# The prompt's output projection and final norm, moved from the attention of the samples to the end of the input projections

## The chip, the cores and the metric

The kernel runs on one core of one Trainium2 chip. The metric is device time in microseconds of a whole call. In the text PE is the matrix engine (TensorE), PEld its weight load, DVE the vector engine, ACT the scalar engine, POOL GpSimd, and SP the engine whose queue issues nearly all DMAs here.

## The reference

Two layers work on 256 prompt rows and 2048 sample rows of width 1024. Layer 0 is a convolution, layer 1 attention. What matters here is the end of layer 1 for the prompt:

```
q, k, v, z = split(h @ na_w_in)                     # prompt: 256 rows, sample: 2048 rows
att  = context_attention(q, k, v)                   # prompt, 16 heads of 64
out  = (att * silu(z)) @ na_w_out                   # 1024 x 1024 weights
x    = x + gate * out                               # gate of the prompt: from c_ctx
y_prompt = rms_norm(x, final_g)
# the sample rows: the same with neighbourhood attention and another gate
y_sample = rms_norm(x_s + gate_s * ((att_s * silu(z_s)) @ na_w_out), final_g)
```

Everything is f32. A product of two f32 matrices is made of three f32r matmuls: each operand is split into a rounded half (h) and the rest (l), and h\*h, h\*l and l\*h are added up in PSUM.

## The kernel before

**Stages.** `phase1` does layer 0, the input projections of layer 1 (`na_values`, `na_rest`) and the attention of the prompt (`prompt_attention`). `phase2` does the attention of the samples (`attention`) with the output projections woven in. Intermediate results go through scratch in HBM: queries `qh_d`/`ql_d`, keys `ks_d`, the SiLU branch `zn_d`, the prompt's gated attention `yp_d`, and the gated, split output weights `w2_d`.

**The end of the input projections.** `na_rest` yields 24 parts (eight column blocks `ct`, in each a key, a query and a SiLU part, numbered 1, 0, 3). A part is 24 matmuls of 128x512 on each of two blocks of 512 rows and 24 of 128x256 on a block of 256 rows. In profile rows these matmuls are `ni_s`, lines L356 to L358. Their PSUM bank is emptied by ACT (`ni_s_f`, `ni_s_h`), and the results are stored by SP from a ring of six `st` tiles.

**What is woven in there.** `weave` and `mixed` set the order in which the program is written: beside eight parts run the generators `prompt_attention` (eight pairs of heads, tiles `pa_*`, the last store is `yp_d<-pa_yl`), `gated_weights` and `context_values` (tiles `cv`). `gated_weights` reads `na_w_out`, multiplies it by both gates (DVE), rounds it (ACT), takes the rest (DVE) and stores four quarters for each of eight row blocks and two gates into `w2_d`. A scheduler then moves instructions within this stretch, by the estimates that it makes of each engine; the order of each engine is fixed in the program, and SP's DMAs are issued in that order.

**The hand-over.** When the prompt's attention is done, its memory is given back, and `start_attention` loads the first two heads of the samples (`a_k`, `a_bm`, `a_qh`, `a_ql`, `ck`, `cv`, `a_v`, `a_z`) while the last three parts of `na_rest` are computed.

**phase2.** 64 heads (two halves `hg` of eight heads, four groups `G` of 512 rows) of four units each make 256 units. A unit has four score matmuls (`sa_S`), softmax, eight transposes (`sa_T`), and in every second unit the product with the values (`sa_O`). PE and DVE keep the order that `attention` writes. `out_group` is the output projection of a group: for each tile of 128 rows and each half of the columns 12 matmuls, in two chunks of six; `side_chunk` puts one chunk into a unit where there is one in `chunks`. The weights are read from `w2_d` into `w2h`/`w2l` by `load_w2` (1 MB each, four buffers), the first ones at the steps W2_STEPS. At step BEGIN = 20 two groups for the prompt (`G` is None) come ahead of all others: they read `yp_d` (`yp_0h`, ...), use their own weights, and the weights of the samples are loaded after them. `while self.tiles_left + nt > 7` in `head_out` empties the list of chunks at once when too many tiles wait. Where PE's names in the order below have `sa_3_1_S`, this is head 3, unit 1 of a group.

Of the kernel before, what the change touches and what calls it, by code (L numbers as in the profile page):

```python
# [18 lines left out]
P = 128  # L19
D = 1024  # L20
# [28 lines left out]
BEGIN = 20  # L49
WAIT = 3  # L50
NEAR = 3
W2_STEPS = 8, 14
# [24 lines left out]
class Kern:  # L77
    def __init__(self, ctx, tc, io):
        self.tc, self.nc, self.io = tc, tc.nc, io
        self.ctx = ctx  # L80
        self.more, self.turn = None, 0
# [16 lines left out]
        self.w2_d = d("w2_d", [2, 2, D, D])  # L98
# [25 lines left out]
    def mm_bank(self, name, tag="mm"):  # L124
        if self.more and tag == "mm":
            self.turn = (self.turn + 1) % 3
            if self.turn:
                return self.more.tile([P, 512], F32, tag=tag, name=name, bufs=4)
        return self.ps.tile([P, 512], F32, tag=tag, name=name)
# [1021 lines left out]
    def gated_weights(self):  # L1151
# [3 lines left out]
        gate = [self.spread_row(work(f"gate1_{g}"), self.gate_d[1, g]) for g in range(2)]  # L1155
        for k in range(NK):
# [3 lines left out]
            for g in range(2):  # L1160
                for i in range(2):
                    cs = slice(512 * i, 512 * i + 512)
                    t, hi = (self.bp.tile([P, 512], dt, tag="out", name=f"w2_{k}{g}{i}{s}", bufs=4) for dt, s in ((F32, "t"), (F32R, "h")))
                    lo = t.bitcast(F32R)
                    nc.vector.tensor_tensor(out=t, in0=raw[:, cs], in1=gate[g][:, cs], op=ALU.mult)
                    nc.scalar.copy(hi, t)
                    self.rest_dve(lo, t, hi)
                    nc.sync.dma_start(self.w2_d[g, 0, rows, cs], hi.bitcast(F32))
                    nc.sync.dma_start(self.w2_d[g, 1, rows, cs], lo.bitcast(F32))
                    yield  # L1170
# [99 lines left out]
    def phase1(self):  # L1270
        tc = self.tc
        with ExitStack() as c:
# [34 lines left out]
            with tc.tile_pool(name="bp", bufs=1, side="right") as self.bp:  # L1307
                with tc.tile_pool(name="mb", bufs=1, side="right") as self.mb, tc.tile_pool(name="more", bufs=1, space=bass.MemoryType.PSUM) as self.more:
                    side = itertools.chain(self.context_keys(), self.masked_bias())
# [57 lines left out]
    def attention(self):  # L1367
# [10 lines left out]
        for i in range(-1, len(units) + 4):  # L1378
            self.step = i
            if i in W2_STEPS:  # L1380
                self.load_w2(0, 0, W2_STEPS.index(i), True)
            if i == BEGIN:
                for hg in range(2):
# [384 lines left out]
```

## Time and profile before

| | |
|---|---|
| median of 3 runs | 2831.47 us (2831.18 to 2834.06) |
| the profiled execution's own time | 2833.08 us |
| its span, first to last instruction | 2831.3 us |
| mean granted clock of PE | 0.985 |
| PE busy / DVE / ACT / POOL | 95% / 65% / 51% / 53% of the span |
| DMA | 548.02 MB, mean 194 GB/s |
| first score matmul of the samples (start of phase2 on PE) | 1822.96 us |

The page gives the busy time of each engine, the span in 40 slices with the granted clock and the DMA share, the chain of work that ended last, and the costliest groups of instructions. The views used below are the table of stretches (busy microseconds of each engine in a stretch, then the granted clock, the share of the 16 DMA engines, and GB/s), the list of waits (engine and line, who released it, microseconds in total, times, longest), the instructions in order of time (start, duration, engine, line), the groups by line (count, busy microseconds, mean ns, idle time before) and the chain.

### The profile page before, as it was taken

The numbers are of one execution on the slowest core, as the hardware profiler recorded it, in microseconds if no ns is written. First come the engines' busy times: TensorE is split into PE (matmuls) and PEld (weight loads), VectorE is DVE, ScalarE is ACT, GpSimd is POOL, SyncE is SP. The second block draws the span as 40 slices with busy tenths as digits, with TensorE's granted clock in tenths as the row PEclk, the third lists the DMA queues.
The fourth block names the chain that finished last, engine by engine and source line by source line (L and its number), as shares of the span: only waits on it lengthen the run. The fifth ranks groups of instructions, "written<-read, shape, count | busy, mean of one in ns | idle before, by whom it ended". The sixth has DMA issues, their size and how long they took to land.

```text
span 2831.3 us, 45475 instructions
## 1 busy us (share of the span) xinstructions
PE 2694.4 (95%) x16079; PEld 2329.6 (82%) x16079; DVE 1851.7 (65%) x3154; ACT 1450.6 (51%) x2546; POOL 1505.6 (53%) x1631
## 2 busy tenths in 40 slices
PE   6999999999899999999999989989899999899998
PEld 4888877776677888999998878778788898788887
DVE  4789989999886510023456542277487787778885
ACT  4457565677544312233212254266476676667774
POOL 5679878888663343354213334145455555455564
PEclk9999999999899999999999999999999999999999
DMA  7233554555435554446789996799777767966753
GB/s 255 84 119 113 188 179 159 188 177 181 155 120 165 165 157 129 132 144 224 238 295 348 342 298 213 199 239 240 225 207 198 198 181 197 247 189 180 199 168 109
DMA packets 435627, 548.02 MB, mean 194 GB/s; under 512 B 42945, under 2 KB 306201, under 8 KB 435272
## 3 DMA queue, kind: packets, MB, share of 16 engines
q1 hardware_dynamic: 430080, 522.17, 61.9%
q10 hardware_dynamic: 5320, 22.95, 2.1%
q8 instruction: 128, 2.10, 0.3%
q14 instruction: 99, 0.81, 0.1%
HBM read 359.86 MB, written 189.22 MB: 194 GB/s over the span
## 4 chain that ended last, share of the span: by engine, by line
PE 67%; DMA 12%; DVE 7%; SPq 4%; ACT 4%; POOL 2%; issue 2%; POOLq 0%; ACTq 0%; DVEq 0%
PE sa_T L1527 7%; PE ci_ps L356 6%; PE ci_ps L357 6%; PE ci_ps L358 6%; PE sa_O L1556 5%; PE sa_O L1551 4%; PE sa_S L1495 3%; PE sa_S L1494 3%; PE ni_s L356 3%; PE ni_s L357 3%; PE ni_s L358 3%; PE o L1658 2%; PE o L1660 2%; PE o L1659 2%; DVE cv L507 2%
## 5 line engine op out<-in xcount | busy, mean ns | idle before, releaser
L1521 POOL TENSOR_SCALAR sa_p<-sa_p,sa_m 128x992 f32<-128x992 f32 (+2 forms) x256 | 279.2, 1091 | 442.2 <-DVE sa_m L1520 319.0
L507 DVE SCALAR_TENSOR_TENSOR cv<-u,dw,cv 128x640 f32<-128x640 f32 (+2 forms) x570 | 427.8, 821 | 3.8 <-ACT cv L503 2.9
L1536 ACT CAST sa_pt<-sa_T 128x512 fp32r<-128x512 f32 (+3 forms) x512 | 275.3, 588 | 224.9 <-PE sa_T L1527 223.3
L112 DVE TENSOR_TENSOR sa_pt<-sa_T,sa_pt 128x512 fp32r<-128x512 f32 (+3 forms) x512 | 328.4, 682 | 3.3 <-ACT sa_pt L1536 3.0
L356 PE MATMUL ci_ps<-h_s_hi,ci_wh 128*128 128x512 f32 x768 | 306.6, 399 | 1.8 <-DVE shift L244 1.0
L358 PE MATMUL ci_ps<-h_s_hi,ci_wl 128*128 128x512 f32 x768 | 303.1, 395 | 0.0
L357 PE MATMUL ci_ps<-h_s_lo,ci_wh 128*128 128x512 f32 x768 | 302.7, 394 | 0.0
L1513 DVE TENSOR_REDUCE sa_m<-sa_S 128x1 f32<-128x512 f32 x256 | 176.1, 688 | 190.0 <-PE sa_S L1495 175.3
L1519 ACT ACTIVATE sa_p<-sa_S,sa_m 128x992 f32<-128x992 f32 (+2 forms) x256 | 267.3, 1044 | 56.1 <-DVE sa_m L1515 47.6
L1527 PE MATMUL sa_T<-ident,sa_p 128*128 128x128 f32 (+3 forms) x2048 | 272.6, 276 | 9.1 <-DVE sa_pt L112 8.7
L1527 PEld LDWEIGHTS sa_T<-ident,sa_p 128*128 128x128 f32 (+3 forms) x2048 | 239.3, 138 | 44.8 <-issue 14.0
L488 POOL TENSOR_TENSOR cv_s<-cv_s,cv_p 128x519 f32<-128x519 f32 (+1 forms) x155 | 233.3, 1505 | 69.6 <-DVE cv_s L511 46.9
L485 ACT ACTIVATE cv_p<-u,dw 128x640 f32<-128x640 f32 (+2 forms) x326 | 241.0, 770 | 55.0 <-POOL cv_s L488 35.8
L488 POOL TENSOR_TENSOR cv_p<-cv_p,cv_p 128x520 f32<-128x520 f32 (+1 forms) x155 | 227.8, 1470 | 26.6 <-ACT cv_p L485 18.9
L1556 PE MATMUL sa_O<-sa_pt,a_v 120*128 120x256 f32 (+5 forms) x1280 | 190.2, 278 | 0.0
L1551 PE MATMUL sa_O<-sa_pt,cv 128*128 128x256 f32 x1024 | 175.2, 293 | 3.6 <-ACT sa_pt L1536 0.8
L356 PEld LDWEIGHTS ci_ps<-h_s_hi,ci_wh 128*128 128x128 f32 x768 | 145.4, 189 | 39.1 <-ACT cv_p L485 2.5
L1515 DVE CUSTOM_DVE_ANT_0 sa_S<-sa_S,a_bm,sa_m 128x480 f32<-128x480 f32 (+2 forms) x256 | 170.9, 668 | 9.1
L358 PEld LDWEIGHTS ci_ps<-h_s_hi,ci_wl 128*128 128x128 f32 x768 | 144.9, 189 | 33.6
L357 PEld LDWEIGHTS ci_ps<-h_s_lo,ci_wh 128*128 128x128 f32 x768 | 145.2, 189 | 31.0
L1556 PEld LDWEIGHTS sa_O<-sa_pt,a_v 120*128 120x128 f32 (+2 forms) x1280 | 167.0, 191 | 0.0
L356 PE MATMUL ni_s<-h_s_hi,nis_wh 128*128 128x512 f32 x384 | 151.2, 394 | 8.4 <-DVE ni_s_l L112 5.4
(849 smaller groups left out, 7186.4 us busy)
## 6 DMA issues: line engine op xcount, KB each, us to landing
adaw<-in_ada_w SPq DMA_DIRECT2D x24, 1024.0 KB
ci_w<-in_conv_w_in SPq DMA_DIRECT2D x48, 512.0 KB
a_bm<-bm_d SPq DMA_DIRECT2D x32, 720.0 KB
x_s<-in_x_sample SPq DMA_DIRECT2D x32, 512.0 KB
vs_d<-v_s SPq DMA_DIRECT2D x128, 128.0 KB
a_qh<-qh_d SPq DMA_DIRECT2D x128, 128.0 KB
a_ql<-ql_d SPq DMA_DIRECT2D x128, 128.0 KB
o_x<-x_d SPq DMA_DIRECT2D x32, 512.0 KB
```

Of the source, the lines that this page charges most:

```text
L112: self.nc.vector.tensor_tensor(out=lo, in0=src, in1=hi.bitcast(F32), op=ALU.subtract)
L356: self.nc.tensor.matmul(out, wh[:, k, :], hh[:, k, :], start=k == 0, stop=False)
L357: self.nc.tensor.matmul(out, wh[:, k, :], hl[:, k, :], start=False, stop=False)
L358: self.nc.tensor.matmul(out, wl[:, k, :], hh[:, k, :], start=False, stop=k == NK - 1)
L488: nc.gpsimd.tensor_tensor(out=st["sum", half], in0=st["sum", half], in1=st[half, tap], op=ALU.add)
L507: nc.vector.scalar_tensor_tensor(out=out, in0=u, scalar=w, in1=first, op0=ALU.mult, op1=ALU.add)
L1519: nc.scalar.activation(p[:, n], S[:, n], AF.Exp, scale=-1.0, bias=m[:, 2:3], accum_out=m[:, 3:4])
L1521: nc.gpsimd.tensor_scalar(out=p[:, n], in0=p[:, n], scalar1=m[:, 3:4], scalar2=1.0, op0=ALU.mult, op1=ALU.mult)
L1527: nc.tensor.transpose(t[:w, c * P : c * P + P], p[:, x + c * w : x + c * w + w], self.ident)
L1536: nc.scalar.copy(pt[:w, 0, part, :, at], t)
L1551: nc.tensor.matmul(o, cv[:, c].rearrange("p s d -> p (s d)"), x, start=s + c == 0, stop=False)
L1556: nc.tensor.matmul(dst, v[:w, c0 + c].rearrange("p s d -> p (s d)"), loc[:, lo:hi], start=False, stop=s == 1 and c == 3)
```

## The change

The two prompt groups leave `phase2`. A new generator, `prompt_out`, does the prompt's whole output projection, residual and final norm in `phase1`, right behind `prompt_attention`, beside two parts of `na_rest`. It reads `na_w_out` itself in 16 pieces of 128x512, gates and splits each on the way (`gated`: DVE, ACT, DVE) and multiplies at once, so `gated_weights` makes and stores only the samples' weights. The prompt's attention is woven into six parts in place of eight. The first weights of the samples are loaded at steps 14 and 22 in place of the prompt's at 8 and 14.

```diff
-BEGIN = 20
-W2_STEPS = 8, 14
+W2_STEPS = 14, 22
...
-            self.turn = (self.turn + 1) % 3
+            self.turn = (self.turn + 1) % (1 + self.more_bufs // 2)
...
     def gated_weights(self):
...
-            for g in range(2):
-                for i in range(2):
...
+            for i in range(2):
+                cs = slice(512 * i, 512 * i + 512)
+                t, hi = (self.bp.tile([P, 512], dt, tag="out", name=f"w2_{k}{i}{s}", bufs=4) for dt, s in ((F32, "t"), (F32R, "h")))
+                self.gated(t, hi, t.bitcast(F32R), raw[:, cs], gate[:, cs])
+                nc.sync.dma_start(self.w2_d[0, rows, cs], hi.bitcast(F32))
+                nc.sync.dma_start(self.w2_d[1, rows, cs], t)
+                yield
+    def gated(self, t, hi, lo, raw, gate):
+        self.nc.vector.tensor_tensor(out=t, in0=raw, in1=gate, op=ALU.mult)
+        self.nc.scalar.copy(hi, t)
+        self.rest_dve(lo, t, hi)
+    def prompt_out(self, pool, ps):
+        nc, io = self.nc, self.io
+        T = lambda tag, dt, n, bufs, name="": pool.tile([P, n], dt, tag=tag, name=f"po_{tag}{name}", bufs=bufs)
+        gate = self.spread_row(T("gate", F32, D, 1), self.gate_d[1, 0])
+        fg = self.spread_row(T("fg", F32, D, 1), io["final_g"])
+        y, x = [], []
+        for k in range(NK):
+            t = pool.tile([P, 2, NPR], F32R, tag="y", name=f"po_y{k}", bufs=NK)
+            nc.sync.dma_start(t.bitcast(F32), self.yp_d[k].rearrange("s p t -> p s t"))
+            y.append(t)
+        todo = [(h, k) for h in range(2) for k in range(NK)]
+        def weights(h, k):
+            cs = slice(h * 512, h * 512 + 512)
+            raw, t, hi, lo = (T(tag, dt, 512, bufs, f"{h}{k}") for tag, dt, bufs in (("raw", F32, 3), ("t", F32, 2), ("hi", F32R, 3), ("lo", F32R, 3)))
+            nc.sync.dma_start(raw, io["na_w_out"][0, k * P : k * P + P, cs])
+            self.gated(t, hi, lo, raw, gate[:, cs])
+            return hi, lo
+        ahead = [weights(*todo.pop(0)) for _ in range(2)]
+        for u in range(2):
+            x.append(T("x", F32, D, 2, str(u)))
+            nc.sync.dma_start(x[u], self.x1_d[u * P : u * P + P, :])
+        yield
+        for h in range(2):
+            cs = slice(h * 512, h * 512 + 512)
+            pm = [ps.tile([P, 512], F32, tag="po", name=f"po_{h}{u}", bufs=2) for u in range(2)]
+            for k in range(NK):
+                wh, wl = ahead.pop(0)
+                for u in range(2):
+                    yh, yl = (y[k][:, s, u * P : u * P + P] for s in range(2))
+                    nc.tensor.matmul(pm[u], yh, wh, start=k == 0, stop=False)
+                    nc.tensor.matmul(pm[u], yh, wl, start=False, stop=False)
+                    nc.tensor.matmul(pm[u], yl, wh, start=False, stop=k == NK - 1)
+                yield
+                if todo:
+                    ahead.append(weights(*todo.pop(0)))
+                yield
+            for u in range(2):
+                nc.vector.tensor_tensor(out=x[u][:, cs], in0=pm[u], in1=x[u][:, cs], op=ALU.add)
+            yield
+        for u in range(2):
+            r = self.rms_scale(x[u], f"po_n{u}")
+            nc.vector.scalar_tensor_tensor(out=x[u], in0=x[u], scalar=r, in1=fg, op0=ALU.mult, op1=ALU.mult)
+            nc.sync.dma_start(io["y_prompt"][0, u * P : u * P + P, :], x[u])
+        yield
...
-                    side = self.mixed(self.prompt_attention(pq, pps), side, 40 / 52)
-                    self.weave(itertools.islice(rest, 8), side, 14.5)
+                    side = self.mixed(self.prompt_attention(pq, pps), side, 24 / 52)
+                    self.weave(itertools.islice(rest, 6), side, 13)
                     for _ in side:
                         pass
             extra.close()
+            with tc.tile_pool(name="po", bufs=1, side="right") as po, tc.tile_pool(name="pops", bufs=1, space=bass.MemoryType.PSUM) as pps, tc.tile_pool(name="more2", bufs=1, space=bass.MemoryType.PSUM) as self.more:
+                self.more_bufs = 2
+                side = self.prompt_out(po, pps)
+                self.weave(itertools.islice(rest, 2), side, 18)
+                for _ in side:
+                    pass
+            self.more = None
             self.start_attention()
...
-            if i == BEGIN:
-                for hg in range(2):
-                    self.chunks.append(self.out_group({"hg": hg, "G": None}))
-                    self.due += 4 * NPR // P + WAIT
-                    self.tiles_left += NPR // P
```

**SP, end of the prompt's attention.** Before (line 1244 stores `yp_d`, lines 1450 and on load the first head of the samples):

```order
L1244 DMA yp_d<-pa_yh 128x256
L1087 DMA ql_d<-ni_0_s_l 128x4x64
L1244 DMA yp_d<-pa_yl 128x256
L1011 DMA zn_d<-ni_3_s_f 128x512
L1450 DMA a_0_k<-ks_d 128x704
L1455 DMA a_0_bm<-bm_d 128x3x352
L1459 DMA a_0_qh<-qh_d 64x512 x2
```

The same place in the changed program, and what stands there ahead of the samples' first load (lines 1294, 249, 1183, 1190 and 1503 are `yp_d`, gate, `yp_d` read back, `na_w_out` and the first head):

```order
L1294 DMA yp_d<-pa_yl 128x256
L249 DMA po_gate<-gate_d 128x1024
L249 DMA po_fg<-in_final_g 128x1024
L1183 DMA po_y_16729<-yp_d 128x2x256
...
L1190 DMA po_raw_17049<-in_na_w_out 128x512
L1010 DMA zn_d<-ni_3_s_f 128x512 x2
L1219 DMA out_y_prompt<-po_x_16761 128x1024
L1219 DMA out_y_prompt<-po_x_16763 128x1024
L1010 DMA zn_d<-ni_3_s_f 128x256
L1503 DMA a_0_k<-ks_d 128x704
```

Between the last store of the prompt's attention and the samples' first load stand now the 30 DMAs of `prompt_out` and ten stores of the projections.

**ACT, last column block of the projections.** Before, the SiLU parts that empty PSUM (line 1010) follow one another:

```order
L1010 ACTIVATE ni_3_s_f<-ni_3_s_16888 128x256
L1010 ACTIVATE ni_3_s_f<-ni_3_s_16967 128x512
L1010 ACTIVATE ni_3_s_f<-ni_3_s_16995 128x512
L1010 ACTIVATE ni_3_s_f<-ni_3_s_17023 128x256
L1106 CAST ni_1_s_h<-ni_1_s_17057 128x512
```

In the changed program (line 1170 rounds the prompt's weights, line 257 squares its rows for the norm, line 1009 is the SiLU):

```order
L1009 ACTIVATE ni_3_s_f<-ni_3_s_16943 128x256
L1170 CAST po_hi_16789<-po_t_16788 128x512
...
L1170 CAST po_hi_17051<-po_t_17050 128x512
L257 ACTIVATE po_n_sq,po_n_r<-po_x_16761 128x1024
L257 ACTIVATE po_n_sq,po_n_r<-po_x_16763 128x1024
L1009 ACTIVATE ni_3_s_f<-ni_3_s_17135 128x512
L1009 ACTIVATE ni_3_s_f<-ni_3_s_17163 128x512
```

The banks 17135 and 17163 of the last SiLU part are emptied only behind the prompt's last 13 weights and the squares of its norm. On PE the third block of that part, bank 17191, comes right behind the last matmul of `prompt_out`, and the SiLU part has two banks:

```order
L1207 MATMUL po_16972<-po_lo_17052,po_y_16743 128x512
L1208 MATMUL po_16972<-po_hi_17051,po_y_16743 128x512
L355 MATMUL ni_3_s_17191<-h_s_hl,nis_7_3_wh 128x256
L356 MATMUL ni_3_s_17191<-h_s_hl,nis_7_3_wh 128x256
```

Of the 96 prompt matmuls 48 stand in this order in a row behind the second block of that part; the other 48 are mixed with projection matmuls.

**PE in phase2.** In units 24 to 37 the eight prompt chunks of the first half are gone. Of the second half, 12 are gone from units 43 and 44, and of the 66 matmuls of unit 45 there remain 30, those of the samples' group 0. Nothing else in the order of PE in phase2 differs.

More of the change, by code (lines that the diff above doesn't have):

```diff
@@ L80, in __init__ @@
         self.ctx = ctx
-        self.more, self.turn = None, 0
+        self.more, self.more_bufs, self.turn = None, 0, 0
         self.cp = ctx.enter_context(tc.tile_pool(name="consts", bufs=1))
@@ L125, in mm_bank @@
         if self.more and tag == "mm":
-            self.turn = (self.turn + 1) % 3
+            self.turn = (self.turn + 1) % (1 + self.more_bufs // 2)
             if self.turn:
-                return self.more.tile([P, 512], F32, tag=tag, name=name, bufs=4)
+                return self.more.tile([P, 512], F32, tag=tag, name=name, bufs=self.more_bufs)
         return self.ps.tile([P, 512], F32, tag=tag, name=name)
@@ L1154, in gated_weights @@
         work = lambda name: self.xp.tile([P, D], F32, tag="ln", name=name, bufs=5)
-        gate = [self.spread_row(work(f"gate1_{g}"), self.gate_d[1, g]) for g in range(2)]
+        gate = self.spread_row(work("gate1"), self.gate_d[1, 1])
         for k in range(NK):
@@ L1159, in gated_weights @@
             nc.sync.dma_start(raw, self.io["na_w_out"][0, rows, :])
-            for g in range(2):
-                for i in range(2):
[L1162 to L1170, printed above, removed]
+            for i in range(2):
[5 more added lines that the diff above has]
+                yield
@@ L1601, in head_out, with load_w2 @@
             self.put_off(3 + u, lambda u=u: split(u))
-    def load_w2(self, hg, g, h, hold=False):
-        if hg > 1:
-            return
-        w = [self.T("w2", [P, 4, 512], F32R, f"w2{s}{hg}{g}{h}") for s in "hl"]
+    def load_w2(self, hg, h, hold=False):
+        w = [self.T("w2", [P, 4, 512], F32R, f"w2{s}{hg}{h}") for s in "hl"]
         for s in range(2):
-            src = self.w2_d[g, s, hg * 512 : hg * 512 + 512, h * 512 : h * 512 + 512]
+            src = self.w2_d[s, hg * 512 : hg * 512 + 512, h * 512 : h * 512 + 512]
             if hold:
@@ L1613, in load_w2 @@
             self.nc.sync.dma_start(w[s].bitcast(F32), src.rearrange("(k p) n -> p k n", p=P))
-        self.w2.setdefault((hg, g), []).append(w)
+        self.w2.setdefault(hg, []).append(w)
     def out_group(self, grp):
         nc, T, hg, G = self.nc, self.T, grp["hg"], grp["G"]
-        g = 0 if G is None else 1
-        w = self.w2[hg, g]
+        w = self.w2[hg]
         if hg and self.fg is None:
             self.fg = self.spread_row(T("row", [P, D], F32, "final_g"), self.io["final_g"])
-        out = self.io["y_prompt" if G is None else "y_sample"][0]
-        base = 0 if G is None else NPR + G * 512
-        o0 = 0 if G is None else G * 512
-        if G is None:
-            grp["y"] = [tuple(T("y", [P, 4, P], F32R, f"yp{hg}_{u}{s}") for s in "hl") for u in range(NPR // P)]
-            for u, y in enumerate(grp["y"]):
-                for s, t in enumerate(y):
-                    self.hold(t[:, 0, 0:1])
-                    nc.sync.dma_start(t.bitcast(F32), self.yp_d[4 * hg : 4 * hg + 4, s, :, u * P : u * P + P].rearrange("c p t -> p c t"))
-        if G is None or G == 0:
+        out = self.io["y_sample"][0]
+        base = NPR + G * 512
+        o0 = G * 512
+        if G == 0:
             for _ in range(WAIT):
```

9 lines of the change are left out of this document (5 added, 4 removed).

## The prediction

> **What bounds the kernel now.** I read the page first, then stretches around the two places that the change touches, then the waits in them.
>
> ```profile
> PE 2694.4 (95%) x16079; PEld 2329.6 (82%) x16079; DVE 1851.7 (65%) x3154; ACT 1450.6 (51%) x2546; POOL 1505.6 (53%) x1631
> ```
>
> PE is the bound, so a matmul that is only moved is worth nothing by itself. A gain must come from PE's idle time, and the table of stretches shows where there is some.
>
> ```profile
> 1620.00:1740.00 120.00, 105.22 (x577) 89.77 (x576) 44.47 (x74) 57.76 (x130) 40.93 (x50) 0.97 0.90 286
> 1740.00:1820.00 80.00, 80.00 (x437) 69.61 (x436) 13.69 (x22) 20.12 (x40) 24.45 (x28) 1.00 0.69 189
> 1955.50:2035.00 79.50, 64.33 (x352) 52.04 (x350) 39.19 (x83) 35.85 (x65) 30.88 (x38) 0.94 0.85 245
> ```
>
> The reader sees the duration, the busy time of PE first, and at the end clock, DMA share and GB/s. Where the prompt's attention runs (1620 to 1740) PE idles 14.8 us under nearly full DMA engines; behind it, where the output projection now goes, PE has no hole. In phase2 between 1955.5 and 2035 it idles 15.2 us. The waits name the causes:
>
> ```profile
> PE ni_s L356 <- DVE ni_s_l L112: 5.4, 2, 3.2
> PE ni_s L356 <- ACT ni_s_f L1010: 3.7, 1, 3.7
> ...
> PE o_None L1658 <- DMA yp_0h<-yp_d: 5.6, 1, 5.6
> PE o L1659 <- DMA w2l<-w_d: 2.1, 1, 2.1
> ```
>
> The first two are of 1615 to 1740 (emptying of PSUM, held up behind stores), the last two of 1955 to 2035: the prompt's second half waits for its data, and the samples' group for weights that load only when the prompt's are done with. These two causes leave the program.
>
> **What phase2 gives back.** Units are counted by `sa_S` (four each), output matmuls by `w2h` (two of three). Three tables over the same stretches: all engines, `sa_S`, `w2h`.
>
> ```profile
> 1833.70:1858.10 24.40, 23.05 (x171) 20.72 (x169) 21.57 (x54) 18.27 (x35) 8.73 (x9) 1.00 0.75 199
> 1903.60:1955.40 51.80, 51.08 (x345) 45.96 (x344) 41.63 (x94) 34.95 (x65) 26.37 (x40) 1.00 0.86 220
> 1966.50:2098.30 131.80, 117.48 (x704) 99.78 (x703) 81.52 (x170) 72.46 (x131) 59.28 (x78) 0.96 0.79 221
> 2115.40:2215.60 100.20, 99.53 (x656) 88.49 (x655) 77.83 (x169) 67.75 (x123) 51.39 (x70) 1.00 0.68 184
> 2468.00:2571.50 103.50, 100.72 (x656) 88.18 (x655) 80.98 (x169) 70.74 (x127) 55.70 (x75) 1.00 0.65 179
> ...
> 1833.70:1858.10 24.40, 8.10 (x32) 1.00 0.75 199
> 1903.60:1955.40 51.80, 14.68 (x56) 1.00 0.86 220
> 1966.50:2098.30 131.80, 31.18 (x108) 0.96 0.79 221
> 2468.00:2571.50 103.50, 30.56 (x108) 1.00 0.65 179
> ...
> 1903.60:1955.40 51.80, 11.63 (x32) 1.00 0.86 220
> 1966.50:2098.30 131.80, 36.57 (x96) 0.96 0.79 221
> 2468.00:2571.50 103.50, 23.29 (x64) 1.00 0.65 179
> ```
>
> First term. Units 24 to 37 (1903.6 to 1955.4, 14 units) hold 48 prompt matmuls. Without them they are like units 4 to 11 (1833.7 to 1858.1), which hold no output chunk: 24.4 / 8 = 3.05 us each, 14 x 3.05 = 42.7, a gain of 9.1. The matmuls themselves would be 11; the rest stays, since DVE is then busy 21.57 of 24.40 us. Bounds: 0, if loads set the pace there (below), to 9.1.
>
> Second term. Units 41 to 67 (27 units) take 131.8 us with 144 output matmuls. The changed program has 96 there, in the same pattern as units 169 to 195 of the second half (103.5 us, one burst of 30, first chunks of a group): a gain of 28.3. Against the 27 units at 2115.4 (100.2 us) it is 31.6, but those have no burst, so I take 28.3. It holds 11 us of matmuls, the idle time and the slower clock behind it (0.96 against 1.00).
>
> Sum for phase2: -37.4 us (bounds -28.3 and -40.7). The prompt's emptying, adds, squares and scales on ACT, POOL and DVE, its `yp` and weight loads, its stores and its x loads leave with it; their cover was PE, so they add nothing. What is late next is the pace of DVE and PE themselves.
>
> **What phase1 pays.**
>
> ```profile
> 1717.36 0.39 PE L356 MATMUL ni_s<-h_s_hi,nis_wh 128*128 128x512 f32 x1
> 1720.08 0.39 PE L356 MATMUL ni_s<-h_s_hi,nis_wh 128*128 128x512 f32 x1
> 1727.33 0.58 PE L356 MATMUL ni_s<-h_s_hl,nis_wh 128*128 128x256 f32 x1 [3.69 <-ACT ni_s_f L1010]
> 1729.84 0.41 PE L358 MATMUL ni_s<-h_s_hl,nis_wl 128*128 128x256 f32 x1
> 1730.23 0.28 PE L357 MATMUL ni_s<-h_s_hl,nis_wh 128*128 128x256 f32 x1
> 1730.91 0.28 PE L357 MATMUL ni_s<-h_s_hl,nis_wh 128*128 128x256 f32 x1
> ```
>
> (1) Matmuls: twelve of 128x512 start within 2.72 us, 0.227 each; 96 x 0.227 = +21.8, with no idle PE to cover them. Six of 128x256 take 0.68 us when warm (0.113), and 11 take 2.51 right behind a gap of 3.69 us: such a gap costs another 1.3 us.
>
> (2) The first prompt matmul. It needs the last pair's `yp_d` landed, then gate, norm weights, eight `y` and a piece of weights, through SP in this order.
>
> ```profile
> 1766.89 0.64 PE L1231 MATMUL pa_O<-pa_pt,pa_v 128*128 128x256 f32 x4
> ...
> 1773.79 0.32 SPq L1244 DMA_DIRECT2D yp_d<-pa_yl  x1
> 1775.64 0.32 SPq L1450 DMA_DIRECT2D a_k<-ks_d  x1
> ...
> 1801.26 0.47 SPq L1115 DMA_DIRECT2D ks_d<-ni_s_h  x1
> ...
> 1822.96 0.50 PE sa_S L1494
> ```
>
> From the last `pa_O` (end 1767.53) to the load behind the landing are 8.1 us. The loads are 2 x 0.52 + 8 x 0.26 = 3.1 MB, 11.0 us at the 286 GB/s above; the weights 0.9 more; multiplication 0.71 and rounding 0.62 (rows below) 1.3: 21.3 us. The new order of PE has 72 matmuls of 128x512 and 39 of 128x256 between the two: 16.3 + 4.4 = 20.7. A wait of 0.6; I take 1 (0 to 10, the upper end when each step doubles its row: not sooner). SP's issues lie under the transfers: in the rows above it issues 24 loads of the samples and five stores in 25.6 us.
>
> (3) The stream of weights. Three `raw` buffers: a piece can be had each (landing + 1.3) / 3. PE uses one in six matmuls, 1.36 us; in the second 48 nothing covers it.
>
> ```profile
> L1165 DVE TENSOR_TENSOR w_510t<-w,gate 128x512 f32<-128x512 f32 x1 | 0.7, 707 | 3.6 <-DMA w_d<-w_500h 3.6
> L1146 ACT CAST cv<-cv 128x512 fp32r<-128x512 f32 x8 | 4.7, 617 | 11.5 <-DMA cv<-in_cache_v 11.2 <-DVE w_701t L1165 0.4
> ...
> 702.22 3.66 DMA co_raw<-in_conv_w_out
> ...
> 1682.84 8.50 DMA cv<-in_cache_v
> 1713.74 6.19 DMA cv<-in_cache_v
> ```
>
> The rows of the chain are landings of 512 KB, quiet and crowded; a piece is 256 KB. At 3.66 us: 1.65 per piece, 8 x 0.29 = 2.3; at 8.50: 3.27, 8 x 1.9 = 15. Beside it the DMA share is like 1740 to 1820 (0.69), so the quiet row is nearest: +2 (0 to 15). DVE's two passes per piece, 1.4 us, keep pace with PE. On SP the stores of the SiLU part are queued behind pieces that wait for a `raw` buffer; their `st` tiles are wanted again only at the hand-over (5), so nobody waits for them here. The DVE and ACT work of gating is as much as before, half of it moved here, beside matmuls.
>
> [...]
>
> (4) ACT's order. The third block of the last SiLU part waits for a bank that ACT empties behind the prompt's two squares.
>
> ```profile
> L1679 DVE TENSOR_TENSOR o_x<-o,o_x 128x512 f32<-128x512 f32 x9 | 6.2, 688 | 3.8 <-PE o L1660 3.7
> ...
> L258 ACT ACTIVATE o_sq<-o_x 128x1024 bf16<-128x1024 f32 x6 | 6.3, 1056 | 20.9 <-DVE o_x L1679 20.9
> L258 ACT ACTIVATION_READ_ACCUMULATOR o_sq<-o_x 128x1 f32 x6 | 1.1, 187 | 0.0
> ```
>
> From the last prompt matmul: one add 0.7, two squares 2 x 1.24, one SiLU of the size of the rounding 0.6: 3.8 us of wait, and 1.3 of slow clock: +5 (3 if the first add starts early).
>
> [...]
>
> (5) The hand-over. Before, the samples' first loads took SP from 1775.64 to 1801.26, 25.6 us, with 47 us of projections left (to 1822.96). Now they are issued about 8 us behind the last prompt matmul (squares, scales, two stores), the `ks_d` stores behind them at about 34 us, and PE has 3.8 + 2.7 + 13.6 + 10.9 = 31 us until it needs a bank whose ACT copy waits for those stores (ring of six `st`): a wait of about 3. +3 (0 to 9).
>
> (6) Less DMA in the tail. 32 stores of 256 KB fewer, 8.4 MB, 29 us of DMA at 286 GB/s; the loads and stores of `cv`, which stand in the chain at 1683 and 1714 ahead of PE's waits, come earlier. The idle 14.8 us and 3.6 of slow clock (120 x 0.03) can go: at most -18; the prompt's attention, in six parts now, keeps its own dependences. I take -10 (-4 to -18).
>
> Sum for phase1: 21.8 + 1 + 2 + 5 + 3 - 10 = +22.8. With phase2: -14.6. Against the profiled execution's own 2833.1 that is 2818.5; the median of runs is 1.6 lower, so 2817.
>
> **Rivals.** A, slower: the DMA engines stay full through the prompt's projection. Place: the second 48 matmuls. Price: weights landing in 8.50 us cost 15 instead of 2, the first wait 10 instead of 1, and the tail is relieved of 4 instead of 10: -14.6 + 13 + 9 + 6 = +13, 2845. At a landing of 6.19 it is (2.5 - 1.36) x 8 = 9, with half of the others about +0: between the two it decides. For it speaks the share of 0.90 up to 1740; against it 0.69 behind, and the stores that go.
>
> B, no change: phase2 gives back less. The first weights of the samples come at steps 14 and 22, into units without output matmuls, where heads are used faster.
>
> ```profile
> PE sa_S L1494 <- DMA ck<-kc_d: 6.3, 1, 6.3
> ```
>
> This wait, between 1860 and 1900, comes behind the two pairs of weight loads of steps 8 and 14. If loads set the pace in units 14 to 37, 7 of the first term's 9.1 stay and such a wait comes once more: -14.6 + 7 + 6.3 = -1, 2830.
>
> C, much faster: terms 2, 3 and 5 are hidden, term 6 is 18, and phase2 gives 40.7: 21.8 + 5 - 18 - 40.7 = -32, 2800.
>
> That the work stays in phase2 or is pulled elsewhere is excluded by the order shown.
>
> **How the numbers follow.** The likeliest case 0.60, A 0.10, B 0.15, C 0.15. The range 2802 to 2834 leaves out A and the far half of C, and takes in B. A measurement of this kernel tells about 0.2% (5.7 us) from no change: the likeliest case and C are faster (0.75), B is the same (0.15), A slower (0.10).
>
> **What would show it.** In the profile after: the first `sa_S` about 23 us later than 1822.96; from it to the end 37 us less than before; no wait of PE for `yp`, and 27 units from the 41st in about 103 us (term two); 14 units from the 24th in 43 us (term one); a wait of PE's `ni_s` of about 4 us behind the last `po` matmul, released by ACT (term 4); PE's waits in the tail below 5 us (term 6); landing of the weights in the second 48 matmuls (term 3). It is wrong if PE waits for `po_hi` or `po_lo` again and again, or if the units from 24 on wait for loads.

## The result, and the profile after

The changed kernel takes 2819.59 us (median of six runs, 2811.96 to 2821.11) against 2833.55 us for the kernel before on the same chip: a ratio of 0.9945, 95% interval 0.9931 to 0.9959. The forecast was 2817 within 2802 to 2834, so the time came out as forecast. Two of its steps did not come out where they were said to, and the profile shows which. The profiled execution took 2820.92 us (span 2819.1 us).

The engines' line of the page of the changed kernel:

```profile
PE 2692.4 (96%) x16079; PEld 2328.8 (83%) x16079; DVE 1849.1 (66%) x3150; ACT 1446.6 (51%) x2538; POOL 1488.6 (53%) x1623
```

PE has the same 16079 matmuls as before and, within 2 us, the same busy time; what went is for the most part idle time. Some instructions of the changed kernel on PE in order of time: the first of the 96 prompt matmuls, the first and the last of the second 48, then the projection behind them, the last wait of the projections, and the first score matmul of the samples.

```profile
1772.37 0.63 PE L1206 MATMUL po<-po_hi,po_y 128*128 128x512 f32 x2
...
1795.35 0.39 PE L1206 MATMUL po<-po_hi,po_y 128*128 128x512 f32 x1
...
1806.02 0.39 PE L1208 MATMUL po<-po_hi,po_y 128*128 128x512 f32 x1
...
1809.44 0.38 PE L355 MATMUL ni_s<-h_s_hl,nis_wh 128*128 128x256 f32 x1 [3.03 <-ACT ni_s_f L1009]
...
1842.19 0.58 PE L355 MATMUL ni_s<-h_s_hl,nis_wh 128*128 128x256 f32 x1 [3.55 <-ACT ni_s_f L1017]
...
1848.24 0.51 PE L1547 MATMUL sa_S<-ck,a_qh 128*128 128x512 f32 x1 [0.55 <-ACT ni_s_f L1017]
...
1938.89 0.77 PE L1547 MATMUL sa_S<-ck,a_qh 128*128 128x512 f32 x1 [5.38 <-DMA ck<-kc_d]
```

The first `sa_S` comes at 1848.24 us in place of 1822.96: 25.3 us later. From there to the end of the span it is 970.9 us in place of 1008.3: 37.4 us less. The second 48 prompt matmuls start within 10.67 us, 47 steps of 0.227, without a wait. The next two rows show two waits of PE that the kernel before did not have, and the last one a wait for context keys.

Stretches of the changed kernel (duration, busy time of PE first, at the end clock, DMA share and GB/s). The third begins at the last matmul of `na_values`, which stands ahead of all that the change touches on PE, and ends at the first `sa_S`; the last three are units 0 to 23, 24 to 37 and 41 to 67:

```profile
1500.00:1620.00 120.00, 113.90 (x593) 97.55 (x592) 74.18 (x102) 31.71 (x52) 36.91 (x24) 1.00 1.00 355
1620.00:1740.00 120.00, 118.14 (x683) 104.10 (x682) 37.74 (x64) 55.84 (x129) 51.77 (x68) 1.00 0.79 233
1453.65:1848.24 394.59, 379.50 (x2020) 328.16 (x2018) 172.00 (x254) 124.15 (x244) 122.66 (x120) 0.99 0.84 268
1848.24:1920.96 72.72, 65.09 (x453) 57.37 (x453) 61.11 (x151) 51.65 (x95) 32.80 (x49) 0.98 0.89 240
1920.96:1972.11 51.15, 43.52 (x298) 38.27 (x296) 40.78 (x92) 33.21 (x61) 21.33 (x35) 0.93 0.86 213
1983.17:2086.74 103.57, 100.78 (x657) 88.21 (x655) 78.16 (x169) 68.05 (x123) 51.77 (x70) 1.00 0.66 180
```

Two stretches of the kernel before that the prediction did not show, for the first and the third row:

```profile
1500.00:1620.00 120.00, 119.84 (x633) 103.43 (x632) 79.39 (x112) 31.32 (x52) 39.60 (x28) 1.00 1.00 347
1449.06:1822.96 373.90, 358.40 (x1924) 308.67 (x1922) 167.50 (x248) 121.33 (x240) 121.93 (x116) 0.99 0.88 283
```

The reader sees three things. In the tail (1620 to 1740) PE idles 1.9 us in place of 14.8 and the clock is 1.00 in place of 0.97. Ahead of it (1500 to 1620) it idles 6.1 us in place of 0.2. And measured from a point that both programs reach in the same way, the end of the projections costs 394.6 - 373.9 = 20.7 us; the other 4.6 of the 25.3 had passed ahead of that point (1453.65 against 1449.06). It came at anything from 1449 to 1457 us in the 13 profiles of this case, with the same order of PE up to it, so a single span can't be read closer than that.

### The profile page after: what moved, and what is told of

The parts are those of the page before. It is cut to its first block, busy times and chain, and to the rows that moved or that the text cites. A ratio compares the mean times of both kernels' runs of the same rounds, so it can differ in the third digit from the quotient of the medians.

```text
span 2819.1 us, 45421 instructions
## 1 busy us (share of the span) xinstructions
PE 2692.4 (96%) x16079; PEld 2328.8 (83%) x16079; DVE 1849.1 (66%) x3150; ACT 1446.6 (51%) x2538; POOL 1488.6 (53%) x1623
## 4 chain that ended last, share of the span: by engine, by line
PE 69%; DMA 10%; DVE 7%; SPq 4%; ACT 3%; POOL 3%; issue 2%; POOLq 0%; ACTq 0%; DVEq 0%
PE sa_T L1580 7%; PE ci_ps L355 6%; PE ci_ps L356 5%; PE ci_ps L357 5%; PE sa_O L1609 5%; PE sa_O L1604 4%; PE sa_S L1548 4%; PE sa_S L1547 4%; PE ni_s L356 4%; PE ni_s L357 4%; PE ni_s L355 4%; DMA bm_d<-bm 2%; PE o L1702 2%; PE o L1704 2%; PE o L1703 2%
```

## The experiments

Lines of rows can differ by up to nine between these kernels, since the edits add lines.

**One: the samples' weights later.** Units 24 to 37 lost 5.4 us to a wait for `ck` behind the weight loads. Do they collide, or do all loads together set the pace?

```diff
-W2_STEPS = 14, 22
+W2_STEPS = 30, 36
```

> The changed kernel with the samples' first weights at steps 30 and 36 in place of 14 and 22, nothing else. Theory (a collision): only the first group of heads loads context keys, and the wait of 5.4 us for ck in unit 27 comes because four loads of 1 MB stand ahead of those keys on the queue; behind the last key they meet nothing. Then the waits for ck in units 19 and 27 (1.1 and 5.4 us) are gone, units 0 to 37 take 117 to 118 us in place of 123.9, and the run is 6 to 7 us shorter, about 2813. Rival (the pace of all loads, rival B of the prediction): the bytes of units 14 to 45 are the same, so a wait of 4 us or more comes back in units 28 to 46 for keys, queries or w2h, and the time stays within 2 us of 2819.6.

2818.58 us, ratio 0.9943 (0.9928 to 0.9957). The total can't tell it from the changed kernel, and the 6 to 7 us of the expectation did not come; the profile tells them apart. Units 24 to 37 of this kernel, and the only wait of PE for a load from the first `sa_S` up to 1990 us:

```profile
1919.20:1966.38 47.18, 43.02 (x297) 37.82 (x295) 41.08 (x98) 33.26 (x62) 23.27 (x39) 0.96 0.97 244
```

```profile
PE sa_S L1548 <- DMA a_ql<-ql_d: 2.0, 1, 2.0
```

The wait for `ck` is gone. So is the 1.1 us of unit 19, which the expectation put down to `ck` and the profile to ACT (`sa_pt`); it had cost nothing, since units 0 to 23 take 72.7 us in both. Units 0 to 37 take 119.9 us in place of 123.9: 4.0 won, not 6 to 7, because 2.0 come back as a wait for queries in unit 36, behind the first pair of weights. So it was a collision for the most part, and the pace of the loads for the rest.

**Two: the old steps.** This separates the two constants from the removal of the prompt's chunks.

```diff
-W2_STEPS = 14, 22
+W2_STEPS = 8, 14
```

> The changed kernel with the steps 8 and 14 of the kernel before in place of 14 and 22. It separates the two constants from the removal of the prompt's chunks. Theory (the wait for ck follows the weights): a wait of about 6 us is back in unit 19 and one of 1 to 1.5 in unit 15, units 0 to 23 take 80 us again (72.7 with steps 14 and 22), units 24 to 37 take 43 to 45 us as the prediction's first term said, and the sum of units 0 to 37 is 123 to 126, the total 2819 to 2822. Rival (the removal made the wait, the steps have no part in it): units 0 to 23 stay at 73, units 24 to 37 at 51.

2810.52 us, ratio 0.9916 (0.9899 to 0.9933). Units 0 to 23 and 24 to 37, and the wait for keys:

```profile
1839.38:1918.25 78.87, 66.68 (x452) 59.49 (x453) 61.52 (x151) 51.64 (x95) 32.78 (x49) 0.94 0.90 244
1918.25:1963.19 44.94, 41.82 (x298) 36.16 (x295) 40.38 (x92) 33.26 (x61) 21.34 (x35) 1.00 0.79 205
```

```profile
PE sa_S L1547 <- DMA ck<-kc_d: 6.5, 2, 5.5
```

The wait is back in unit 19 (5.5 us), units 24 to 37 take 44.9, and the sum is 123.8, as with steps 14 and 22. The steps only choose in which of the two stretches the same wait falls. The total, 9 us below the changed kernel, was not expected (2819 to 2822 was): phase2 as a whole took only 2.2 us less (968.7). Experiments nine and ten come back to it.

**Three: the norm's squares on DVE.** Is the wait of 3.03 us behind the last prompt matmul ACT's order?

```diff
-            r = self.rms_scale(x[u], f"po_n{u}")
+            r = self.rms_dve(x[u], f"po_n{u}")
...
+        nc.vector.tensor_tensor_reduce(junk, xt, xt, 1.0, 0.0, ALU.mult, ALU.add, accum_out=r)
```

> The changed kernel with the two squares of the prompt's norm on DVE (one pass with a sum) in place of ACT. Theory (term 4: PE's wait of 3.03 us behind the last po matmul is ACT's order): the wait is gone, the granted clock of 1800 to 1820 is 1.00 in place of 0.91, and the first sa_S comes 3 to 4.5 us earlier than 1848.24; total about 2816. Rival (the hand-over takes it back): the samples' loads and the stores of keys on SP start when the norm is done, not when PE is, so PE's wait for a bank at 1842 grows from 3.55 to 6 or 7 us, and the first sa_S moves by less than 1 us.

2820.61 us, ratio 0.9941 (0.9922 to 0.9961). Nothing is won. The stretch behind the last prompt matmul, with the squares on ACT (the changed kernel) and then on DVE, and then PE's longest wait from 1760 us to the first `sa_S` with them on DVE:

```profile
1800.00:1820.00 20.00, 16.97 (x80) 14.49 (x79) 7.55 (x10) 5.84 (x11) 2.44 (x4) 0.91 0.42 145
```

```profile
1800.00:1820.00 20.00, 20.00 (x101) 17.04 (x100) 11.99 (x17) 5.04 (x9) 3.48 (x4) 1.00 0.24 89
```

```profile
PE ni_s L364 <- ACT ni_s_f L1026: 9.3, 1, 9.3
```

The theory and its rival hold, one after the other. The wait of 3.03 us and the slow clock behind it are gone, so ACT's order was their cause. But the wait at the hand-over grew from 3.55 to 9.26 us, by more than the 3.03 taken away, and the first `sa_S` came no earlier. What bounds the end of the projections then comes behind the norm on SP; experiment five tests that.

**Four: the prompt's weights stored again.** This prices term 6 by itself; the DVE and ACT passes that fill the stores come back with them.

```diff
+        self.w2p_d = d("w2p_d", [2, D, D])
...
+            for g in range(2):
...
+                    dst = self.w2_d if g else self.w2p_d
+                    nc.sync.dma_start(dst[0, rows, cs], hi.bitcast(F32))
+                    nc.sync.dma_start(dst[1, rows, cs], t)
```

> The changed kernel with the 32 gated and split stores of 256 KB for the prompt (8.4 MB, with their DVE and ACT passes) put back beside its attention; nobody reads them. It prices term 6 of the prediction by itself. Theory (stores were what held up the tail): PE's idle time between 1500 and 1760 grows by 8 to 18 us, released by ACT and DVE behind stores, and the run is as much longer, 2828 to 2838. Rival (the tail was relieved by writing it in six parts, not by fewer stores): below 3 us, 2819 to 2823.

2830.43 us, ratio 0.9985 (0.9972 to 0.9997): 11 us slower than the changed kernel. The two stretches of the tail, and the largest wait of PE between 1640 and 1760 (in all, times, longest):

```profile
1500.00:1620.00 120.00, 120.00 (x634) 103.74 (x634) 78.56 (x112) 31.21 (x51) 39.29 (x28) 1.00 1.01 348
1620.00:1740.00 120.00, 109.39 (x607) 93.44 (x606) 47.67 (x79) 61.80 (x141) 46.27 (x58) 0.97 0.92 294
```

```profile
PE ni_s L356 <- ACT ni_s_f L1018: 3.9, 3, 1.6
```

The idle time of the tail is back (10.6 us, clock 0.97), and that of 1500 to 1620 is gone (0.0). A likely reason for the second stands in the stores of `cv`, which follow `gated_weights` in the same chain: their rows in the kernel before and in the changed kernel (count, shortest, median and longest issue in ns, first and last start).

```profile
L1148 SPq DMA_DIRECT2D cvs_d<-cv x8: 363/608/1802, 1663.8 to 1724.2; - x8
```

```profile
L1147 SPq DMA_DIRECT2D cvs_d<-cv x8: 382/698/930, 1546.8 to 1612.5; - x8
```

With half of the gating gone, the `cv` work comes some 115 us earlier, into a stretch where the DMA engines are full before as after (1.00, 347 and 355 GB/s); in experiment four it is back at 1663.2 to 1727.5. So the stores and their passes cost the tail 8.7 us of idle time and the clock (0.97), which is what the prediction said, and a part of the relief is paid ahead of it. Over 1500 to 1760 us as a whole the idle time is 10.6 us, against 8.0 in the first profile of the changed kernel, so the growth of 8 to 18 that the expectation put there did not come, though the time did. From the last matmul of `na_values` to the first `sa_S` this kernel takes 401.9 us, 7.3 more than that profile and 10.4 more than the mean of the five profiles with the changed kernel's phase1 (those of the changed kernel and of experiments one, two, nine and ten). How large the part ahead is, is not settled: the 6.1 us of idle time in 1500 to 1620 are the most of all profiles. The nine others of kernels that store one set of weights have 2.1 to 4.6 there, the three that store two have 0.2 at most. That the `cv` work is what makes PE wait there is not shown; the profile puts these waits down to ACT and DVE, which empty the banks (4.7 and 1.4 us in the changed kernel).

**Five: a shorter hand-over.** Only the first head is loaded ahead of the last stores of keys.

```diff
-        self.load_ahead(1)
-        for h in range(NEAR):
-            self.load_context(self.sequence[0].ctx, h)
+        self.load_ahead(0)
```

> The changed kernel with fewer loads at the hand-over: start_attention loads only the first head of the samples (9 DMAs in place of 24); the second head and the contexts are loaded by phase2, as all later heads are. The orders of PE, ACT, DVE and POOL stay as they are; on SP four stores of keys now come right behind the nine loads. Theory (term 5: PE's last wait of 3.55 us in the projections is SP's queue, 24 loads between the norm and the stores of keys): the first ks_d store is issued about 15 x 0.65 = 10 us earlier than 18 us behind the first load, the wait falls below 0.5 us, and from the first pa_S to the first sa_S it is 190 us in place of 193 to 196; the wait of 3.03 us for ACT stays. Rival (the bytes set it, DMA share 1.05 in 1820 to 1840): the second head's loads land too late, PE waits 4 us or more in units 4 to 8, and nothing is won.

2817.74 us, ratio 0.9935 (0.9916 to 0.9954). SP in order of time, first load of the samples and first store of keys, in the changed kernel and then in this one:

```profile
1815.05 0.33 SPq L1503 DMA_DIRECT2D a_k<-ks_d  x1
...
1832.98 3.06 SPq L1114 DMA_DIRECT2D ks_d<-ni_s_h  x1
```

```profile
1815.66 0.33 SPq L1501 DMA_DIRECT2D a_k<-ks_d  x1
...
1820.93 1.10 SPq L1114 DMA_DIRECT2D ks_d<-ni_s_h  x2
```

From the first `pa_S` to the first `sa_S`, and then units 0 to 23:

```profile
1653.12:1842.64 189.52, 184.07 (x1010) 160.11 (x1008) 63.73 (x103) 76.13 (x164) 62.95 (x80) 0.99 0.70 207
1842.64:1917.20 74.56, 66.08 (x452) 58.08 (x453) 61.27 (x151) 51.45 (x95) 32.76 (x49) 0.95 0.93 247
```

The stores come 5.3 us behind the first load in place of 17.9, the wait of 3.55 us is gone, and the stretch takes 189.5 (192.5 to 195.6 in those five profiles). Term 5's cause is shown. Units 0 to 23 give 1.8 of it back, 1.5 of that in unit 2, and the total can't tell this kernel from the changed one.

**Six: three edits together,** those of one, three and five.

> Three edits on the changed kernel: the squares on DVE (experiment three, where the wait moved to the hand-over), the short hand-over, and the weights at steps 30 and 36. Theory (the two waits at the end of the projections are one chain through SP, and each edit alone shifts it): now both go, from the first pa_S to the first sa_S it is 186 to 188 us (195.6 in the changed kernel, 197.0 with the squares alone), from the first sa_S to the end 966 to 969; the run takes about 2809. Rival (a third wait stands behind: the norm itself, from the last po matmul to the samples' loads): the first sa_S waits for a_k or ck instead, 192 us or more, 2815.

2810.06 us, ratio 0.9910 (0.9890 to 0.9930). The same two stretches, and ACT's first cast of the samples' transposed scores:

```profile
1650.60:1834.79 184.19, 182.32 (x1010) 158.68 (x1008) 66.01 (x107) 73.96 (x160) 63.98 (x80) 1.00 0.69 207
1834.79:1918.31 83.52, 68.38 (x452) 60.23 (x453) 61.46 (x147) 51.34 (x95) 32.78 (x49) 0.90 0.79 204
```

```profile
1852.03 1.07 ACT L1596 CAST sa_pt<-sa_T 128x512 fp32r<-128x512 f32 x2 [9.63 <-DMA a_qh<-qh_d]
```

The stretch of the projections is 11 us shorter (184.2), and units 0 to 23 take 11 us more (83.5): in unit 3 PE waits 8.7 us for this cast and the DVE pass behind it. It is neither of the two places that the expectations named. By the profile the cast waits for a DMA. Phase1's last stores of queries were issued just ahead of it, at 1843.9 and 1844.4, behind the loads of the second head; which of these DMAs it was is not settled. The total came out at the 2809 that was expected, but not by the way: the first stretch is shorter than the 186 to 188 expected, and from the first `sa_S` to the end it takes 977.7 in place of 966 to 969. The profiled execution (2814.29) is the slowest of the four, so the 83.5 need not hold for the others.

**Seven: phase2's half alone.** Phase1 is that of the kernel before, with the stores of experiment four; the prompt's output projection and norm are left out, and one copy fills their place.

```diff
-                side = self.prompt_out(po, pps)
-                self.weave(itertools.islice(rest, 2), side, 18)
...
-                    self.weave(itertools.islice(rest, 6), side, 13)
+                    self.weave(itertools.islice(rest, 8), side, 14.5)
...
+            self.nc.sync.dma_start(self.io["y_prompt"][0], self.x1_d[0:NPR, :])
```

> One half of the change alone: phase2 of the changed kernel behind the phase1 of the kernel before (prompt's attention in eight parts, weights of both gates stored), and no output projection of the prompt at all: y_prompt is filled with rows of x1 by one DMA. It leaves out the 96 matmuls and the norm. Theory (the two halves of the change add up): the first sa_S comes at 1823 plus or minus 5, from there to the end it takes 971 as in the changed kernel, so the run takes 2794 to 2800, 37 us less than before. Rival (phase2 gained from the loads that phase1 finished earlier, or from the weights of the prompt that are no longer stored): from the first sa_S to the end more than 980.

2795.78 us, ratio 0.9861 (0.9842 to 0.9880). From the last matmul of `na_values` to the first `sa_S`, and units 0 to 37 (units 41 to 67 take 103.59):

```profile
1456.32:1827.17 370.85, 358.11 (x1924) 308.35 (x1922) 165.16 (x247) 121.14 (x240) 121.42 (x116) 0.99 0.88 285
1827.17:1951.08 123.91, 108.13 (x747) 95.47 (x747) 101.88 (x242) 84.82 (x155) 54.17 (x84) 0.96 0.84 221
```

From the first `sa_S` (1827.17) to the end of the span (2798.1) it takes 970.9 us, as in the changed kernel. That they agree to the tenth is chance, since a second profile of the changed kernel has 974.0 (experiment nine); that the two halves add up holds within these 3 us.

**Eight: one buffer for the prompt's weights.** Term 3 had no row of a lone load of 256 KB; this makes some.

```diff
-(("raw", F32, 3), ("t", F32, 2), ("hi", F32R, 3), ("lo", F32R, 3))
+(("raw", F32, 1), ("t", F32, 2), ("hi", F32R, 3), ("lo", F32R, 3))
```

> The changed kernel with one raw buffer for the prompt's weights in place of three: a piece can be fetched only when the one before has been multiplied. It measures what term 3 had to guess, the time of one lone load of 256 KB. A piece then takes landing + 0.7 us. PE takes 2.5 us per piece in the first half, where projections are mixed in, and 1.36 in the second. If a load lands in 2 us, the period is 2.7 and the run is 8 x 0.2 + 6 x 1.3 = 10 us longer; at 3.66 (the row of 512 KB in the prediction) 4.4, 15 + 18 = 33 us longer. Theory: three buffers hide any landing up to 3 x 1.36 - 0.7 = 3.4 us, so the measured landing must be below that, and the cost here between 8 and 25 us. Rival (rounding on ACT or the two passes of DVE set the pace, not the load): below 4 us.

2838.94 us, ratio 1.0019 (1.0004 to 1.0034). From the first prompt matmul to the last there are now 54.2 us in place of 33.7, 20.6 more. PE's waits there, one issue, and two multiplications:

```profile
PE po L1206 <- ACT po_hi L1170: 14.7, 10, 1.8
```

```profile
1800.81 0.33 SPq L1190 DMA_DIRECT2D po_raw<-in_na_w_out  x1
...
1803.39 0.69 DVE L1169 TENSOR_TENSOR po_t<-po_raw,po_gate 128x512 f32<-128x512 f32 x1 [1.16 <-DMA po_raw<-in_na_w_out]
...
1807.00 0.69 DVE L1169 TENSOR_TENSOR po_t<-po_raw,po_gate 128x512 f32<-128x512 f32 x1 [1.46 <-DMA po_raw<-in_na_w_out]
```

From issue to multiplication it is 2.6 us, and the period here 3.6, so 2.9 with the multiplication taken off. That is below the 3.4 that three buffers hide by the expectation's estimate (3 x 1.36 - 0.7), and the cost lies within the 8 to 25 of the theory. In the changed kernel the 16 loads of 256 KB, with three buffers, cost PE no wait between its first prompt matmul (1772.37) and its last (1806.02).

**Nine and ten: the changed kernel and the early steps again, side by side.**

> The changed kernel itself once more, unedited, beside the next two on the same chip. Up to the first pa_S its PE program is the same as before's, and in the profiles so far that point came anywhere between 1646 and 1655 us. Theory (drift ahead of the change, different in each execution): the time is 2812 to 2822 again, the first pa_S to the first sa_S 193 to 196, from there to the end 969 to 973. Rival (something of the change itself differs by execution): the stretch between pa_S and sa_S or phase2 moves by more than 4 us.

> The changed kernel with the samples' weights at steps 8 and 14, a second time: its four runs of experiment two were 9 us below those of the changed kernel, though phase2 took only 2.2 us less. Theory (it is the drift ahead of the change): on the same chip as the changed kernel it now comes within 3 us of it. Rival (the early steps are really better): 6 us or more below again, and the profile shows it behind the first sa_S.

2818.84 us, ratio 0.9949 (0.9932 to 0.9966), and 2818.64 us, 0.9944 (0.9926 to 0.9961). Side by side the two are the same; the 9 us of experiment two did not come again. From the last matmul of `na_values` to the first `sa_S`, and units 0 to 37, of the changed kernel a second time:

```profile
1456.27:1849.00 392.73, 379.33 (x2019) 327.50 (x2018) 172.35 (x254) 124.14 (x244) 122.16 (x120) 0.99 0.84 268
1849.00:1972.45 123.45, 108.96 (x746) 95.94 (x747) 101.90 (x242) 84.91 (x155) 54.25 (x84) 0.96 0.89 231
```

These repeat within 2 us, and from the first `pa_S` to the first `sa_S` it is 192.9 in place of 195.6. From the first `sa_S` to the end it takes 974.0 in place of 970.9, a microsecond more than expected. The second profile of the early steps is 9.6 us longer than that of experiment two: 4.4 of them lie ahead of the first `pa_S` (1650.35 and 1645.96), 1.7 from there to the first `sa_S` and 3.5 behind it. So the drift lies for a good part ahead of the change, but not only there, as the expectation had it; what makes it was not looked into.

**Eleven: the norm apart.** Four edits; the new one takes the prompt's rows and the norm's weights out of the memory that the samples wait for.

```diff
-            x.append(T("x", F32, D, 2, str(u)))
+            x.append(self.t4(F32, f"po_x{u}", [P, D]))
...
-        fg = self.spread_row(T("fg", F32, D, 1), io["final_g"])
+        fg = self.spread_row(self.t4(F32, "po_fg", [P, D]), io["final_g"])
```

> Four edits on the changed kernel: squares on DVE, the first head alone at the hand-over, weights at steps 30 and 36, and the rows and the norm's weights of the prompt in tiles of phase1's own (t4), so that the memory for the samples' heads is free at the last po matmul and not at the last store of y_prompt. Theory (experiment six paid its 11 us back in unit 3 because the second head's loads began at 1828; here all loads begin some 8 us earlier): from the first pa_S to the first sa_S 184 to 187 us, no wait above 3.2 us in units 1 to 8, units 0 to 23 in 72 to 75, from the first sa_S to the end 966 to 970; 10 to 13 us less than the changed kernel beside it. Rival (the bytes of the hand-over, two heads and the stores, need 30 us wherever they start): a wait of 4 us or more in units 2 to 8, less than 6 us won.

2804.46 us, ratio 0.9902 (0.9881 to 0.9924), against 2818.84 for the changed kernel beside it on the same chip: 14 us less. From `pa_S` to `sa_S`, units 0 to 23, units 24 to 37, and PE's longest wait from 1750 to 1960:

```profile
1649.47:1834.76 185.29, 182.19 (x1011) 158.48 (x1009) 70.28 (x107) 73.82 (x160) 63.23 (x79) 1.00 0.72 212
1834.76:1909.69 74.93, 65.79 (x453) 57.87 (x453) 61.08 (x147) 51.57 (x95) 34.27 (x51) 0.95 0.81 209
1909.69:1954.94 45.25, 41.43 (x297) 36.36 (x295) 40.70 (x98) 33.23 (x61) 21.66 (x36) 1.00 0.96 244
```

```profile
PE sa_S L1554 <- ACT sa_p L1579: 3.1, 1, 3.1
```

The two stretches that were named are as expected, and so is the one from the first `sa_S` to the end (966.5); the gain of 14 us lies a little above the 10 to 13 expected. The first load of the samples on SP, in experiment six and then here (the last matmul of `prompt_out` starts at 1803.59 and 1801.53):

```profile
1813.85 0.32 SPq L1510 DMA_DIRECT2D a_k<-ks_d  x1
1801.94 0.33 SPq L1510 DMA_DIRECT2D a_k<-ks_d  x1
```

The memory of the prompt's tiles, held until its last store, had kept the samples' loads back: they start 0.4 us behind that matmul in place of 10.3. In these profiles the 8.7 us of unit 3 are gone with it. By the times the step from experiment six to this one is not shown: the ratios 0.9910 (0.9890 to 0.9930) and 0.9902 (0.9881 to 0.9924) overlap. What is shown is that the edits together are faster than the changed kernel (0.9949, 0.9932 to 0.9966).

## Why the prediction was right, step by step

**Phase2, -37.4: measured -37.4** in the changed kernel, and with its half alone; with the second profile of the changed kernel (974.0) it is -34.3, so the agreement to the tenth is luck. The second term (27 units in 103.5 us) came out at 103.57. The first term came out in size, not in place: units 24 to 37 took 51.2 us, not 42.7, and units 0 to 23 72.7 in place of 80.7. The gain over units 0 to 37 is 8.6 us, against 9.1. Units 0 to 23 of the kernel before:

```profile
1822.96:1903.64 80.68, 66.60 (x452) 59.14 (x453) 61.80 (x155) 51.58 (x95) 32.82 (x49) 0.94 0.86 231
```

The step that failed is "without them they are like units 4 to 11": those hold no weight loads, and the steps 14 and 22 put 4 MB ahead of the last context keys. Rival B had seen that wait (6.3) but added it once more; it only moved, from unit 19 to unit 27. Experiment two shows it move back, with 44.9 us in units 24 to 37.

**Phase1, +22.8: measured +20.7** from the last matmul of `na_values` to the first `sa_S`, in the first pair of profiles. Four more profiles have the changed kernel's phase1 (388.2 in experiment two, 390.4 in ten, 391.5 in one, 392.7 in nine), and that of experiment seven has the phase1 before (370.9). All pairs of them give 14.3 to 23.7, on average 19.1. By its terms, in the first pair:

- (1) The matmuls: 0.227 each, as said.
- (2) The first prompt matmul and (3) the weights: no wait, where 1 and 2 were taken. The last of the 16 loads is issued at 1795.3 us, when the second 48 matmuls begin: the loads had run ahead during the first 48. Term 3 was mis-sized by its row, a load of twice the size; a lone piece takes 2.6 to 2.9 us, not 3.66.
- (4) ACT's order: 3.03 us, where 3.8 were said. Behind it 15 matmuls of 128x256 started every 0.213 us in place of 0.113, 1.5 us more: 4.5 together, against 5. The wait is 3.03 in the second profile too, but without slow clock behind it (1.00), so there the term is 3.0.
- (5) The hand-over: the wait was 3.55, where about 3 was said, by the cause that was said. The step left out its slow clock: 23 matmuls behind it at 0.213 cost another 2.3. It is 5.9 in place of 3. In experiments one, two, nine and ten the wait is 2.0 to 4.6.
- (6) Less DMA: idle time in the tail fell by 12.9 and the slow clock's 3.6 us went, near the upper bound of 18; but 5.9 us of new idle time appeared ahead of the tail, where the `cv` work had moved into full DMA engines (2.1 to 4.6 in the other profiles). The net, -10.6, is the -10 of the prediction, by a way that it did not describe. Experiment four puts the price of the stores, with the passes that fill them, at 11 us.

With these the sum is 21.8 + 4.5 + 5.9 - 10.6 = 21.6, against the 20.7 measured in this pair. The terms' own scatter is larger than the difference, so the sum is borne out to some microseconds and no closer. Terms 2 to 4 were 3.5 us too high and term 5 was 2.9 too low in this pair; that they made up for each other is luck.

**The whole.** The first pair gives 20.7 - 37.4 = -16.7; the medians give -14.0 in the first comparison and -16.5 in that of experiment nine. The differences lie within the drift of the stages. Rival A's price (the DMA engines full through the projection) was never paid. The stretch of the second 48 in the changed kernel, PE's prompt matmuls alone:

```profile
1795.30:1806.30 11.00, 10.95 (x48) 1.00 0.10 25
```

The DMA share is 0.10 and PE is busy throughout. Among the first 48, where the weights were still being loaded, PE did not wait either (busy for all of the 22.98 us from 1772.37 to 1795.35).

Terms 4 and 5 were treated as two waits that add up. Experiment three showed that they are one chain: with the first removed (3.03 us) the second grew from 3.55 to 9.26. In experiment six both are gone, since the stores of keys no longer stand on SP behind 24 loads of the samples.

## What to carry to other kernels

The wait for `ck` that came from a burst of loads was not removed here by taking other work away beside it; it followed the burst (5.5 us in unit 19 with the weights at steps 8 and 14 in experiment two, 5.4 in unit 27 with 14 and 22 in the first profile of the changed kernel) and was gone with the steps 30 and 36, so move such a burst behind the last small load that somebody waits for. When two waits stand one behind the other on the way to the same hand-over, removing the first alone can be worth nothing (experiment three: 2820.61 us against 2819.59): look for what the last one hangs on, here the stores of keys behind the samples' loads on one queue (17.9 us behind the first of them, 5.3 in experiment five), and these loads behind the memory that a norm held until its last store (they start 10.3 us behind the last prompt matmul in experiment six, 0.4 in eleven). And the work that was taken out of a queue here pulled forward what was behind it (the stores of `cv`, by some 115 us): ask what the stretch is like into which that moves.

## What the runs showed of the hardware that was not expected

Behind a gap of 3.03 us on PE the slow clock came (0.63 over 4.56 us), though not at once; but it did not come behind every such gap (1.00 over 4.64 us in a second profile). The changed kernel behind its two waits (the clock is the last number but two):

```profile
1809.44:1814.00 4.56, 4.56 (x25) 4.56 (x26) 1.93 (x2) 0.43 (x1) 1.25 (x2) 0.63 0.83 323
1842.19:1847.50 5.31, 5.30 (x24) 5.19 (x24) 0.00 (x0) 0.60 (x1) 3.79 (x4) 0.50 0.74 160
```

Behind the gap of 3.03 us the first eight matmuls still started every 0.11 us or so, and only then 15 at 0.213; behind that of 3.55 us the slow clock (0.50) held for all that was left of the projections, 5 us. The stretch behind the same gap of 3.03 us in the second profile of the changed kernel (1812.36), and then a shorter gap in experiment five, ahead of the tail:

```profile
1812.36:1817.00 4.64, 4.64 (x32) 4.33 (x33) 1.94 (x2) 0.82 (x2) 1.26 (x2) 1.00 0.83 323
```

```profile
1513.83 0.79 PE L355 MATMUL ni_s<-h_s_hi,nis_wh 128*128 128x512 f32 x1 [2.37 <-ACT ni_s_f L1009]
1513.83:1516.55 2.72, 2.72 (x6) 2.14 (x7) 2.72 (x3) 1.38 (x2) 1.76 (x1) 0.50 1.08 384
```

The first had no slow clock behind it (1.00), the second, of 2.37 us, had it at once (0.50 over 2.72 us). So the length of a gap alone did not tell here whether the clock falls, when, or for how long. The gaps are counted from the modelled end of the last matmul; from start to start those of 2.37 and 3.03 are 2.66 and 3.42 us.
